# Weight tiles from one explicit list, two ahead, and the down-projection sums in another stage

## The chip, the core and the metric

The kernel runs on one core of a Trainium2 chip. Its time is the device time of one execution in microseconds (us), the median of several runs. The engines are TensorE (PE, matmuls), VectorE (DVE), ScalarE (ACT), GpSimd (POOL) and SyncE (SP). Here SP issues every DMA, in one queue.

## The reference

One decoder layer on x of 2048 tokens by 1024, in float32:

```python
n = rms_norm(h, norm1_w);  z = n @ w_in            # q, k, v, g_lr, g_out, su, sv
o = gla_chunked(q, k, v, log_a(g_lr))              # 4 heads, chunks of 64, state carried on
o_gla = rms_norm(o, gla_norm_w) * silu(g_out)
o_sg  = gelu(su) * (tril(W_s) @ layer_norm(gelu(sv)) + b)   # chunks of 128
h = h + concat(o_gla, o_sg) @ w_out
n2 = rms_norm(h, norm2_w)
h = h + (silu(n2 @ w_ffn_gate) * (n2 @ w_ffn_up)) @ w_ffn_down   # D_FF = 2816
out = rms_norm(h, final_norm_w)
```

## The kernel before

Tokens are worked in four blocks of 512 (`blk` 0 to 3); two blocks make a pass `s`. A pass runs `mix` and `project` for its first block, the same for its second, then `gate_up` and `down` for both blocks together.

A product in float32 is three matmuls (`mm3`, L112) of operands split in a high and a low part: `split` (L92) makes the high part with a cast on ACT and the low part with a subtraction on DVE. `load_w` (L101) loads a weight tile of 128 x 1024 into one of three raw buffers (`rawp`) and splits it into two of eight buffers (`wp`): four tiles may be there at once.

Large products are done by a scheme with seven block products in place of eight, which needs sums and differences of blocks of both operands. For the value and gate products of blocks 1 to 3 (`pair_product`, L200) the sums of weights are in the DRAM tensor `vd`, those of the activations come from `Halves.make` (L159). For the down projection (`down`, L870) the weight sums are in `td`. For gate and up (`gate_up`, L798) they are made as they are needed (`Weights.prep`), up to six products ahead of the one that PE does (`AHEAD`), in 154 products per pass.

`mix` (L414) does in this order: the first columns of sv with the gate's low rank (`tok_group`), k and q (`col_pair` twice), the rest of sv (`second_half`), v and g_out (two `tok_group` in block 0, `pair_product` in blocks 1 to 3), and su in two pairs (`col_pair`). `project` (L703) multiplies by w_out in two halves of columns. Between the products stand the chunk steps of the linear attention (`chunks`, L520; four per block, each with eight state updates and two masked copies on DVE), the layer norm (`sv_norm`), and the attention's output (`attend`).

The program is written as one stream. Side work is held in generators in the list `bg`, and `tick()` (L66) advances each by one step; it is called after each k tile, in `pair_product` after each of the 14 weight tiles. `finish(g)` runs a generator to its end. From that stream each engine gets a fixed list of instructions, made before the run: an instruction written earlier has precedence, but one written later may be put ahead where its inputs and buffers are free sooner. In the run every engine works through its list in order.

The sums of weights in DRAM are made by `weight_sums` (L389): 15 jobs, four for `vd` and eleven for `td`. Each loads four blocks of 128 x 512, does four subtractions on DVE (L403 to L406) and stores the result (L407). It starts after 8 ticks and then does one job every four ticks, so that it runs beside blocks 0 and 1. Its tiles come from the pool `big` (16 buffers). The pool `nwp` has two buffers of 128 x 1024; it holds norm weights and one temporary of `Halves`.

Before, a tile of weights is loaded where it is used: in `tok_group` at the head of each k step, in `pair_product` by `load(m, kk)`, and for `col_pair` both tiles together ahead of the product. The one tile that is loaded earlier by hand is the first of w_out (`pre`, L695).

Of the kernel before, what the change touches and what calls it, by code (L numbers as in the profile page):

```python
# [8 lines left out]
F32 = mybir.dt.float32  # L9
# [4 lines left out]
ALU = mybir.AluOpType  # L14

P = 128
D = 1024
T = 2048
NB = 512
TT = NB // P  # L20
KD = D // P
# [12 lines left out]
def hybrid_block(ctx, tc, x, norm1_w, w_in, w_gate_up, b_gate_up, gla_norm_w, sg_ln_w, sg_ln_b,  # L34
# [41 lines left out]
    def start(g):  # L76
        bg.append(g)
        return g


    half = const.tile([P, 4], F32, name="half")
# [115 lines left out]
            kh, t = {1: (0, 0), 2: (1, 0), 4: (1, 2)}[m]  # L197
            return self.act(4 * kh + k, (t + th) * P, (t + th + 1) * P)

    def pair_product(load, left, order, bank, drain):  # L200

        acc = {}
        for m in order:
            key = bank[m]
            first = key not in acc
            if first:
                acc[key] = [ps(), ps()]
            for kk in range(2):
                hi, lo = load(m, kk)
                for th in range(2):  # L210
                    for j in range(2):
                        mm3(acc[key][th], left(m, 2 * kk + j, th), (hi[:, j, :], lo[:, j, :]),
                            first and kk + j == 0, kk + j == 2, True)
                    if kk:
                        drain(m, th, acc[key][th])
                tick()

    def row_tiles(u):

# [34 lines left out]
        return load_w([w[k0 * P:(k0 + kk) * P, c0:c0 + c].rearrange("(k p) c -> p k c", p=P) for c0, c in col_list], kk,  # L254
                      sum(c for _, c in col_list))

    def tok_group(w, col_list, act, ks=2, order=None, outer=None, done=None, before=None, ws=None, hook=None, pre=None):

        n = sum(c for _, c in col_list)
        order = order or list(range(0, act.nk, ks))  # L260
        acc = [None] * TT

        def load(k0):
            return tok_load(w, col_list, k0, min(ks, act.nk - k0))

        def products(t, k0, hi, lo):
            if acc[t] is None:
                acc[t] = ps()
            for j in range(hi.shape[1]):
                mm3(acc[t][:, :n], act(k0 + j, t * P, (t + 1) * P), (hi[:, j, :], lo[:, j, :]),  # L270
                    k0 == order[0] and j == 0, k0 == order[-1] and j == hi.shape[1] - 1)

        if outer:
            ws = ws or [load(k0) for k0 in order]
            for ts in outer:
                for k0, (hi, lo) in zip(order, ws):
                    if hook:
                        hook(ts[-1], k0)
                    for t in ts:
                        products(t, k0, hi, lo)  # L280
                for t in ts:
                    done(t, acc[t])
                tick()
        else:
            for k0 in order:
                if before and k0 in before:
                    finish(before[k0])
                hi, lo = pre.pop(k0) if pre and k0 in pre else load(k0)
                for t in range(TT):
                    products(t, k0, hi, lo)  # L290
                    if k0 == order[-1]:
                        done(t, acc[t])
                tick()

    def col_load(w, c0):
        return [load_w([w[k0 * P:(k0 + 4) * P, c0:c0 + 2 * P].rearrange("(k p) c -> p k c", p=P)], 4, 2 * P) for k0 in (0, 4)]

    def col_pair(ws, act, a=0, b=NB):

        acc = [ps(), ps()]  # L300
        for i, (hi, lo) in enumerate(ws):
            for k in range(4):
                for c in range(2):
                    cs = slice(c * P, (c + 1) * P)
                    mm3(acc[c][:, :b - a], (hi[:, k, cs], lo[:, k, cs]), act(4 * i + k, a, b), i + k == 0, i == 1 and k == 3)
            tick()
        return acc
# [78 lines left out]
            nc.tensor.matmul(o, lhsT=ones[0:1, :], rhs=bs_bc[:, g, :], start=False, stop=True)  # L386
        nc.vector.tensor_copy(sgb, pb.rearrange("p (a b) -> p a b", b=P))

    def weight_sums():  # L389

        def blocks(w, r, c):
            return [w[r[i] * P:(r[i] + 1) * P, c[j]:c[j] + 512] for i in range(2) for j in range(2)]

        jobs = [(blocks(w_in, (k, 4 + k), (C_V, C_GOUT)), vd[:, k]) for k in range(4)]
        jobs += [(blocks(w_d, (2 * j, 2 * j + 1), (0, 512)), td[:, j]) for j in range(NF // 2)]
        for _ in range(8):
            yield
        for srcs, dst in jobs:
            t = bigt(F32, "wsum")
            for i, src in enumerate(srcs):  # L400
                nc.sync.dma_start(t[:, i], src)
            b11, b12, b21, b22 = (t[:, i] for i in range(4))
            nc.vector.tensor_tensor(b11, b12, b11, ALU.subtract)  # L403
            nc.vector.tensor_tensor(b12, b22, b12, ALU.subtract)
            nc.vector.tensor_tensor(b22, b22, b11, ALU.subtract)
            nc.vector.tensor_tensor(b21, b21, b22, ALU.subtract)  # L406
            nc.sync.dma_start(dst.rearrange("m p d -> p m d"), t)  # L407
            for _ in range(4):
                yield

    start(constants())
    start(weight_sums())

    def mix(blk, nT, first_w):  # L414

# [53 lines left out]
        g_dec = start(decay())  # L469


        ak = col_pair(col_load(w_in, 256), nT)
        finish(g_dec)
        for p in range(2):
            nc.vector.tensor_tensor(ei[:, p, :], ak[p], ei[:, p, :], ALU.mult)
# [15 lines left out]

        for hh in range(2):
            nc.gpsimd.memset(left[other(hh), hh], 0.0)
        aq = col_pair(col_load(w_in, 0), nT)
        for p in range(2):
            for hh in range(2):
                rows = mine(hh)
# [88 lines left out]

        if halves is None:
            tok_group(w_in, [(C_V, 512)], nT, done=lambda t, acc: nc.scalar.copy(v[:, t, :], acc))
            g_chunks = chunks_start()
            second_half()  # L590
            g_svn = start(sv_norm())
            gw = bigt(F32, "gw")
            tok_group(w_in, [(C_GOUT, 512)], nT, done=gate_done)
        else:
            second_half()
            g_svn = start(sv_norm())
            finish(g_half)
            gw = bigt(F32, "gw")
            right_of = {1: (0, C_V), 2: (4, C_V), 3: (4, C_GOUT)}
            started = []  # L600

            def load(m, kk):
                if m in right_of:
                    k0, c0 = right_of[m]
                    return tok_load(w_in, [(c0, 512)], k0 + 2 * kk, 2)
                i = {5: 0, 7: 1, 4: 2, 6: 3}[m]
                return load_w([vd[i, 2 * kk:2 * kk + 2].rearrange("k p c -> p k c")], 2, 512)

            def drain(m, th, acc):
                lo, hi = th, 2 + th  # L610
                if m == 1:
                    nc.scalar.copy(v[:, lo, :], acc)
                elif m == 2:
                    nc.vector.tensor_tensor(v[:, lo, :], acc, v[:, lo, :], ALU.add)
                elif m == 7:
                    nc.scalar.copy(gw[:, hi, :], acc)
                elif m == 6:
                    nc.scalar.copy(v[:, hi, :], acc)
                elif m == 4:
                    nc.vector.tensor_tensor(v[:, hi, :], acc, v[:, hi, :], ALU.add)  # L620
                    if th:
                        started.append(chunks_start())
                elif m == 5:
                    nc.vector.tensor_tensor(gw[:, hi, :], acc, gw[:, hi, :], ALU.add)
                    nc.scalar.activation(gw[:, hi, :], gw[:, hi, :], AF.Silu)
                    gate_scale(hi)
                else:
                    gate_done(lo, acc)

            pair_product(load, halves, (1, 2, 7, 6, 4, 5, 3), {1: 0, 6: 0, 5: 0, 3: 0, 2: 1, 7: 2, 4: 2}, drain)  # L630
            g_chunks = started[0]
        finish(g_chunks)
        finish(g_svn)
# [56 lines left out]
                split(h, l, mx)  # L690

        for i in range(2):
            ws = col_load(w_in, C_SU + i * 2 * P)
            if i == 1:
                pre = {4: tok_load(w_out, [(0, 512)], 4, 2)}  # L695
            gate_pair(i, col_pair(ws, nT))
        return mixT, g_att, pre, hx

    def residual(hx, dh, acc, t):
        sl = hx[t][:, dh * 512:(dh + 1) * 512]  # L700
        nc.vector.tensor_tensor(sl, acc, sl, ALU.add)

    def project(blk, hx, mixT, g_att, pre, put, outer, ahead=None):  # L703

        def norm2_put(t, xs):
            yield
# [16 lines left out]

        gens = []
        n2w = norm_w(norm2_w[0])
        tok_group(w_out, [(0, 512)], mixT, order=[4, 0, 6, 2], before={0: g_att}, pre=pre, done=lambda t, acc: residual(hx, 0, acc, t))
        tok_group(w_out, [(512, 512)], mixT, outer=outer, done=out_done, hook=hook)
        if not outer:
            start(norm_rows(hx, put, n2w))
# [269 lines left out]
    for s in range(2):  # L999

        blk = 2 * s
        mixT, g_att, pre, hx = mix(blk, nT, first_w)
        first_w = None
        hx1 = dma_x(x2, blk + 1)
        nT = Act(KD, "nT")
# [7 lines left out]
            if t == TT - 1:  # L1013
                nc.sync.dma_start(bd[i], b1[i])

        project(blk, hx, mixT, g_att, pre, put_first, None)
        finish(g_n1)


        blk += 1  # L1020
        mixT, g_att, pre, hx = mix(blk, nT, None)
        b1 = [bigt(F32, f"b1{i}") for i in range(2)]
        b2 = [None, None]
        tm = {}
# [30 lines left out]

        start(first_operands())
        ahead, run = gate_up(s, tm)
        gens = project(blk, hx, mixT, g_att, pre, put_second, ((0, 1), (2,), (3,)), ahead)

        def last_operands():  # L1060
            for g in gens:
# [9 lines left out]

        start(last_operands())
        d_start, d_run = down(s)
        run(d_start())
        tm.clear()

        nxt = {}
# [39 lines left out]
```

## Time and profile before

| | us |
|---|---|
| median of 3 runs | 2050.57 |
| range of the runs | 2049.33 to 2052.22 |
| profiled execution, device time | 2049.34 |
| its span, first to last instruction | 2047.6 |
| PE busy | 1987.0 |
| DVE busy | 1503.1 |
| ACT busy | 892.6 |

A row of the profile names the line, the engine and the operation, what it writes and from what (`wlo<-raw,whi` is the low part of a weight tile). PEclk is the granted clock of TensorE as a share of full speed (2.4 GHz; the other level is 1.2 GHz, shown as 0.5 where it lasts). A matmul's own time is longer than its distance to the next, since matmuls overlap. Because L94, L95 and L115 to L117 are in helpers, rows are told apart by their tiles. In the run, pass 0 has block 0 up to about 200 us, block 1 to 395, gate and up to 815, and down to 1045; the second pass follows in the same order.

### The profile page before, as it was taken

How to read it: one execution, taken by the hardware profiler on the slowest of the kernel's cores; microseconds unless marked ns; L12 is line 12 of the kernel's file. 1: busy time of each engine (PE TensorE's matmuls, PEld its weight loads, DVE VectorE, ACT ScalarE, POOL GpSimd, SP SyncE). 2: the span in 40 equal slices, each digit the busy share in tenths (PEclk: the TensorE clock that was granted, in tenths of full speed). 3: DMA queues.
4: the chain of work that ended last, by engine and by line, in shares of the span. 5: the costliest groups of instructions: out<-in, count | busy, mean ns of one | idle time of the engine just before them, and what ended most of it. 6: DMA issues, size and time to landing. Idle time of an engine off the chain costs nothing. (4 is left out here: it accounts for less than half of the span.)

```text
span 2047.6 us, 26475 instructions
## 1 busy us (share of the span) xinstructions
PE 1987.0 (97%) x9837; PEld 1652.4 (81%) x9837; DVE 1503.1 (73%) x2485; ACT 892.6 (44%) x1454; POOL 88.5 (4%) x102
## 2 busy tenths in 40 slices
PE   7999979999999999999999999999999999999997
PEld 6888967878888888888878788788888888888886
DVE  5677886698877877655797668767987787775466
ACT  4444625354333333443565447345433333334334
POOL 1011100000000000000110001000000000000000
PEclk9999998999999999999999999999999999999999
DMA  6666687423332333865655534723332232367545
GB/s 191 198 215 213 227 266 257 166 98 104 116 104 90 125 101 124 294 199 185 241 172 156 174 105 156 209 99 108 103 124 92 96 122 93 103 213 258 196 160 180
DMA packets 204575, 329.27 MB, mean 161 GB/s; under 512 B 15719, under 2 KB 94237, under 8 KB 203422
## 3 DMA queue, kind: packets, MB, share of 16 engines
q1 hardware_dynamic: 204446, 327.58, 48.8%
q8 instruction: 77, 1.26, 0.3%
q14 instruction: 52, 0.43, 0.1%
HBM read 246.27 MB, written 77.07 MB: 158 GB/s over the span
## 5 line engine op out<-in xcount | busy, mean ns | idle before, releaser
L94 ACT CAST whi<-raw 128x1024 fp32r<-128x1024 f32 (+2 forms) x209 | 210.6, 1010 | 350.0 <-PE ps L116 131.8
L95 DVE TENSOR_TENSOR wlo<-raw,whi 128x1024 fp32r<-128x1024 f32 (+2 forms) x209 | 243.2, 1171 | 141.0 <-ACT whi L94 130.0
L115 PE MATMUL ps<-whi,aop 128*128 128x512 f32 x552 | 215.1, 390 | 0.0
L117 PE MATMUL ps<-whi,aop 128*128 128x512 f32 x552 | 214.9, 389 | 0.0
L116 PE MATMUL ps<-wlo,aop 128*128 128x512 f32 x552 | 214.8, 389 | 0.0
L94 ACT CAST op<-sw 128x512 fp32r<-128x512 f32 x176 | 107.5, 621 | 182.1 <-DVE sw L757 155.3
L95 DVE TENSOR_TENSOR aop<-raw,aop 128x1024 fp32r<-128x1024 f32 x84 | 95.2, 1134 | 96.4 <-ACT aop L94 96.0
L95 DVE TENSOR_TENSOR op<-sw,op 128x512 fp32r<-128x512 f32 x176 | 120.6, 687 | 42.8 <-ACT op L94 42.3
L94 ACT CAST aop<-raw 128x1024 fp32r<-128x1024 f32 x84 | 82.1, 979 | 136.4 <-DMA raw<-ad 135.2
L115 PE MATMUL ps<-whi,nTl 128*128 128x512 f32 (+2 forms) x392 | 128.4, 328 | 3.4 <-DVE nTl L95 3.4
L116 PE MATMUL ps<-wlo,nTh 128*128 128x512 f32 (+2 forms) x392 | 126.6, 323 | 0.2 <-DVE wlo L95 0.2
L117 PE MATMUL ps<-whi,nTh 128*128 128x512 f32 (+2 forms) x392 | 126.6, 323 | 0.0
L116 PEld LDWEIGHTS ps<-wlo,aop 128*128 128x128 f32 x552 | 103.6, 188 | 21.6
L115 PEld LDWEIGHTS ps<-whi,aop 128*128 128x128 f32 x552 | 103.6, 188 | 21.4
L117 PEld LDWEIGHTS ps<-whi,aop 128*128 128x128 f32 x552 | 103.6, 188 | 21.3
L115 PE MATMUL ps<-nTh,wlo 128*128 128x512 f32 x256 | 106.1, 415 | 15.0 <-DVE wlo L95 15.0
L782 ACT COPY p<-ps 128x512 f32<-128x512 f32 x88 | 51.6, 588 | 148.9 <-PE ps L117 143.3
L95 DVE TENSOR_TENSOR op<-raw,op 128x512 fp32r<-128x512 f32 x132 | 88.8, 687 | 31.5 <-ACT op L94 31.0
L122 POOL TENSOR_TENSOR st<-st,half 128x1 f32<-128x1 f32 x48 | 41.6, 875 | 1471.4 <-DVE st L121 1444.8
L115 PE MATMUL ps<-whi,mixTl 128*128 128x512 f32 x256 | 101.9, 398 | 1.8 <-DVE mixTl L95 1.7
L116 PE MATMUL ps<-nTl,whi 128*128 128x512 f32 x256 | 103.4, 404 | 0.0
L117 PE MATMUL ps<-nTh,whi 128*128 128x512 f32 x256 | 103.2, 403 | 0.0
(253 smaller groups left out, 4966.2 us busy)
## 6 DMA issues: line engine op xcount, KB each, us to landing
raw<-ad SPq DMA_DIRECT2D x70, 512.0 KB, 3.8
raw<-in_w_in_dram SPq DMA_DIRECT2D x66, 512.0 KB, 4.6
raw<-in_w_ffn_gate_dram SPq DMA_DIRECT2D x44, 512.0 KB, 3.7
raw<-in_w_ffn_up_dram SPq DMA_DIRECT2D x44, 512.0 KB, 3.8
raw<-td SPq DMA_DIRECT2D x40, 512.0 KB, 4.2
ad<-cg SPq DMA_DIRECT2D x66, 256.0 KB, 2.0
ad<-cs SPq DMA_DIRECT2D x22, 768.0 KB, 3.5
hx<-in_x_dram SPq DMA_DIRECT2D x32, 512.0 KB, 7.1
```

What stands on the lines that cost most here:

```text
L94: nc.scalar.copy(hi, src)
L95: nc.vector.tensor_tensor(lo, src, f32(hi), ALU.subtract)
L115: nc.tensor.matmul(o, lhsT=ll, rhs=rh, start=first, stop=False, skip_group_check=shared)
L116: nc.tensor.matmul(o, lhsT=lh, rhs=rl, start=False, stop=False, skip_group_check=shared)
L117: nc.tensor.matmul(o, lhsT=lh, rhs=rh, start=False, stop=last, skip_group_check=shared)
L122: nc.gpsimd.tensor_tensor(dst, dst, half[:, :k], ALU.pow)
L782: nc.scalar.copy(t[m], o)
```

## The change

Four things are done.

- The weight tiles of a block's `mix` and `project` stand in one list (`block_tiles`), in the order of use, put into `queue` for both blocks of a pass at the pass's start. `next_w()` loads until three tiles are ready and gives out the first, so a tile's load and split are written two tiles ahead of its matmuls, across the borders of products and of the two blocks. `pre` is gone.
- `pair_product` calls `tick()` once for each of its seven block products, not after each of the 14 tiles.
- The value sums (`value_sums`) start after two ticks and take seven ticks a job: one after each load, one after each two subtractions, one after the store.
- The down sums (`down_sums`) are started with the first pass's `gate_up`. There are 22 jobs of half the columns (256), seven ticks each, 154 in all; their tiles come from `nwp`.

```diff
+    AHEAD_W = 2
+    queue, ready = [], []
+    def next_w():
+        while queue and len(ready) <= AHEAD_W:
+            ready.append(queue.pop(0)())
+        return ready.pop(0)
...
 pair_product:
             for kk in range(2):
-                hi, lo = load(m, kk)
+                hi, lo = next_w()
...
-                tick()
+            tick()
...
 tok_group:
-                hi, lo = pre.pop(k0) if pre and k0 in pre else load(k0)
+                hi, lo = ws.pop(0) if ws else next_w()
...
 col_pair:
-        for i, (hi, lo) in enumerate(ws):
+        for i in range(2):
+            hi, lo = next_w()
...
-    def weight_sums():
...
+    def sums_of(t, srcs, dst):
+        for i, src in enumerate(srcs):
+            nc.sync.dma_start(t[:, i], src)
+            yield
+        b11, b12, b21, b22 = (t[:, i] for i in range(4))
+        nc.vector.tensor_tensor(b11, b12, b11, ALU.subtract)
+        nc.vector.tensor_tensor(b12, b22, b12, ALU.subtract)
+        yield
+        nc.vector.tensor_tensor(b22, b22, b11, ALU.subtract)
+        nc.vector.tensor_tensor(b21, b21, b22, ALU.subtract)
+        yield
+        nc.sync.dma_start(dst, t)
+        yield
+    def value_sums():
+        for _ in range(2):
+            yield
+        for k in range(4):
+            srcs = [w_in[r * P:(r + 1) * P, c:c + 512] for r in (k, 4 + k) for c in (C_V, C_GOUT)]
+            yield from sums_of(bigt(F32, "wsum"), srcs, vd[:, k].rearrange("m p d -> p m d"))
+    def down_sums():
+        for j in range(NF // 2):
+            for i in range(2):
+                srcs = [w_d[(2 * j + c) * P:(2 * j + c + 1) * P, l * 512 + i * 256:l * 512 + (i + 1) * 256]
+                        for c in range(2) for l in range(2)]
+                t = nwp.tile([P, D], F32, name="nw", tag="nw").rearrange("p (a b) -> p a b", a=4)
+                yield from sums_of(t, srcs, td[:, j, :, i * 256:(i + 1) * 256].rearrange("m p d -> p m d"))
...
+    OUT_ORDER = [4, 0, 6, 2]
+    VG_ORDER = (1, 2, 7, 6, 4, 5, 3)
+    def block_tiles(blk, first):
...
+        tiles = [] if first else tok_tiles(w_in, first_cols, 3)
+        tiles += col_tiles(w_in, 256) + col_tiles(w_in, 0)
+        second = tok_tiles(w_in, [(C_SV + 256, 256)], 4)
+        if blk == 0:
+            tiles += tok_tiles(w_in, [(C_V, 512)]) + second + tok_tiles(w_in, [(C_GOUT, 512)])
+        else:
+            tiles += second + [lambda m=m, kk=kk: vg(m, kk) for m in VG_ORDER for kk in range(2)]
+        for i in range(2):
+            tiles += col_tiles(w_in, C_SU + i * 2 * P)
+        return tiles + tok_tiles(w_out, [(0, 512)], order=OUT_ORDER) + tok_tiles(w_out, [(512, 512)])
...
     for s in range(2):
         blk = 2 * s
-        mixT, g_att, pre, hx = mix(blk, nT, first_w)
+        queue.extend(block_tiles(blk, first_w) + block_tiles(blk + 1, None))
+        mixT, g_att, hx = mix(blk, nT, first_w)
...
         d_start, d_run = down(s)
+        if s == 0:
+            g_sums = start(down_sums())
         run(d_start())
+        if s == 0:
+            finish(g_sums)
```

## Rows read from the trace of the kernel before

**Rows 1.** The page: busy time, share of the span and instructions of each engine.

```profile
PE 1987.0 (97%) x9837; PEld 1652.4 (81%) x9837; DVE 1503.1 (73%) x2485; ACT 892.6 (44%) x1454; POOL 88.5 (4%) x102
```

**Rows 2.** Table by stage: length, busy time (count) by engine, granted clock, DMA share, GB/s.

```profile
260.00:320.00 60.00, 43.85 (x267) 33.65 (x268) 47.26 (x94) 16.89 (x22) 1.96 (x2) 0.84 0.90 294
...
392.00:440.00 48.00, 45.88 (x197) 36.16 (x197) 45.17 (x74) 29.08 (x53) 1.40 (x2) 0.96 0.47 152
440.00:500.00 60.00, 60.00 (x266) 49.69 (x265) 56.06 (x92) 26.73 (x46) 0.00 (x0) 1.00 0.38 122
500.00:800.00 300.00, 300.00 (x1326) 248.49 (x1325) 230.68 (x365) 109.06 (x189) 0.00 (x0) 1.00 0.33 107
...
1000.00:1056.00 56.00, 51.18 (x279) 44.50 (x278) 50.98 (x91) 35.32 (x71) 11.93 (x14) 0.97 0.69 233
...
1118.00:1146.00 28.00, 23.06 (x163) 17.80 (x164) 23.32 (x51) 7.76 (x10) 0.00 (x0) 0.88 0.78 207
...
1277.00:1330.00 53.00, 48.23 (x302) 38.41 (x302) 41.23 (x82) 20.74 (x26) 2.01 (x2) 0.94 0.68 199
```

**Rows 3.** The same table for two shorter stretches of block 1.

```profile
268.00:278.00 10.00, 6.81 (x23) 5.12 (x22) 6.87 (x10) 4.25 (x7) 0.00 (x0) 0.83 0.70 237
303.00:322.00 19.00, 10.63 (x31) 7.92 (x32) 13.25 (x24) 4.22 (x5) 0.00 (x0) 0.55 0.91 305
```

**Rows 4.** Rows in order of time, PE: start, us, what; in brackets the wait before.

```profile
411.77 0.73 PE L115 MATMUL ps<-t5h,op 128*128 128x512 f32 x2 [1.24 <-ACT t5h L94]
...
1052.70 0.79 PE L115 MATMUL ps<-nTh,wlo 128*128 128x512 f32 x1 [4.82 <-DVE wlo L95]
...
1322.58 0.77 PE L115 MATMUL ps<-nTh,wlo 128*128 128x512 f32 x1 [3.60 <-DVE wlo L95]
```

**Rows 5.** Rows in order of time, DVE, starts of block 2 and end of block 3's product.

```profile
1051.44 1.21 DVE L95 TENSOR_TENSOR wlo<-raw,whi 128x1024 fp32r<-128x1024 f32 x1
...
1302.73 2.99 DVE L536 SCALAR_TENSOR_TENSOR right<-right,dec,ps 64x128 f32<-64x128 f32 x8
1305.64 0.92 DVE L547 COPY_PREDICATED left<-keep,ps 64x256 f32<-64x256 int32 x2
...
1320.02 1.28 DVE L581 TENSOR_TENSOR gw<-gw,gnw 128x512 f32<-128x512 f32 x2
1321.22 3.48 DVE L95 TENSOR_TENSOR wlo<-raw,whi 128x1024 fp32r<-128x1024 f32 x3
```

**Rows 6.** Rows in order of time, ACT, of the same two places.

```profile
1039.69 1.04 ACT L94 CAST whi<-raw 128x1024 fp32r<-128x1024 f32 x1
...
1304.42 1.04 ACT L94 CAST whi<-raw 128x1024 fp32r<-128x1024 f32 x1 [2.97 <-PE ps L116]
```

**Rows 7.** Rows in order of time, SP's queue (DMA issues), block 1.

```profile
223.65 0.34 SPq L88 DMA_DIRECT2D nw<-in_final_norm_w_dram  x1
...
249.51 2.07 SPq L106 DMA_DIRECT2D raw<-vd  x2
...
263.71 1.91 SPq L106 DMA_DIRECT2D raw<-vd  x2
270.90 0.36 SPq L407 DMA_DIRECT2D td<-wsum  x1
```

**Rows 8.** Waits of SP's queue from 200 to 420: us in total, times, longest.

```profile
SPq L407 <- DVE wsum L406: 36.5, 6, 9.1
```

**Rows 9.** One tile, wsum: ns min/median/max, first and last start; the last line is its DMAs'.

```profile
L401 SPq DMA_DIRECT2D wsum<-in_w_ffn_down_dram x44: 418/460/1471, 149.3 to 400.8; - x44
...
L406 DVE TENSOR_TENSOR wsum<-wsum x15: 672/685/693, 70.4 to 411.0; 128x512 f32<-128x512 f32 x15
...
DMA to landing us min/median/max: 3.0/5.3/8.1
```

**Rows 10.** The page's groups: busy us, mean ns of one, idle before.

```profile
L95 DVE TENSOR_TENSOR wlo<-raw,whi 128x1024 fp32r<-128x1024 f32 (+2 forms) x209 | 243.2, 1171 | 141.0 <-ACT whi L94 130.0
...
L95 DVE TENSOR_TENSOR op<-sw,op 128x512 fp32r<-128x512 f32 x176 | 120.6, 687 | 42.8 <-ACT op L94 42.3
```

More of the change, by code (lines that the diff above doesn't have):

```diff
@@ L198, in __call__, with pair_product @@
             return self.act(4 * kh + k, (t + th) * P, (t + th + 1) * P)
-    def pair_product(load, left, order, bank, drain):
+    def pair_product(left, order, bank, drain):
         acc = {}
@@ L255, in tok_load, with tok_tiles, tok_group @@
                       sum(c for _, c in col_list))
-    def tok_group(w, col_list, act, ks=2, order=None, outer=None, done=None, before=None, ws=None, hook=None, pre=None):
+    def tok_tiles(w, col_list, ks=2, order=None):
+        return [lambda k0=k0: tok_load(w, col_list, k0, min(ks, KD - k0)) for k0 in order or range(0, KD, ks)]
+    def tok_group(w, col_list, act, ks=2, order=None, outer=None, done=None, before=None, ws=None, hook=None):
         n = sum(c for _, c in col_list)
@@ L261, in tok_group @@
         acc = [None] * TT
-        def load(k0):
-            return tok_load(w, col_list, k0, min(ks, act.nk - k0))
         def products(t, k0, hi, lo):
@@ L273, in tok_group @@
         if outer:
-            ws = ws or [load(k0) for k0 in order]
+            ws = ws or [next_w() for k0 in order]
             for ts in outer:
@@ L293, in tok_group, with col_tiles, col_pair @@
                 tick()
-    def col_load(w, c0):
-        return [load_w([w[k0 * P:(k0 + 4) * P, c0:c0 + 2 * P].rearrange("(k p) c -> p k c", p=P)], 4, 2 * P) for k0 in (0, 4)]
-    def col_pair(ws, act, a=0, b=NB):
+    def col_tiles(w, c0):
+        return [lambda k0=k0: load_w([w[k0 * P:(k0 + 4) * P, c0:c0 + 2 * P].rearrange("(k p) c -> p k c", p=P)], 4, 2 * P)
+                for k0 in (0, 4)]
+    def col_pair(act, a=0, b=NB):
         acc = [ps(), ps()]
-        for i, (hi, lo) in enumerate(ws):
+        for i in range(2):
+            hi, lo = next_w()
             for k in range(4):
@@ L387, in constants @@
         nc.vector.tensor_copy(sgb, pb.rearrange("p (a b) -> p a b", b=P))
-    def weight_sums():
[L391 to L396, printed above, removed]
-            yield
[L398 to L409, printed above, removed]
@@ L411, in hybrid_block @@
-    start(constants())
-    start(weight_sums())
+    def sums_of(t, srcs, dst):
+        for i, src in enumerate(srcs):
+            nc.sync.dma_start(t[:, i], src)
+            yield
+        b11, b12, b21, b22 = (t[:, i] for i in range(4))
[7 more added lines that the diff above has]
+        yield
@@ new lines, in hybrid_block, with vg @@
+    start(constants())
+    start(value_sums())
+    OUT_ORDER = [4, 0, 6, 2]
+    VG_ORDER = (1, 2, 7, 6, 4, 5, 3)
+    def block_tiles(blk, first):
+        def vg(m, kk):
+            at = {1: (0, C_V), 2: (4, C_V), 3: (4, C_GOUT)}.get(m)
+            if at:
+                return tok_load(w_in, [(at[1], 512)], at[0] + 2 * kk, 2)
+            return load_w([vd[{5: 0, 7: 1, 4: 2, 6: 3}[m], 2 * kk:2 * kk + 2].rearrange("k p c -> p k c")], 2, 512)
+        tiles = [] if first else tok_tiles(w_in, first_cols, 3)
[8 more added lines that the diff above has]
+        return tiles + tok_tiles(w_out, [(0, 512)], order=OUT_ORDER) + tok_tiles(w_out, [(512, 512)])
@@ L469, in mix @@
         g_dec = start(decay())
-        ak = col_pair(col_load(w_in, 256), nT)
+        ak = col_pair(nT)
         finish(g_dec)
@@ L493, in mix @@
             nc.gpsimd.memset(left[other(hh), hh], 0.0)
-        aq = col_pair(col_load(w_in, 0), nT)
+        aq = col_pair(nT)
         for p in range(2):
@@ L598, in mix @@
             gw = bigt(F32, "gw")
-            right_of = {1: (0, C_V), 2: (4, C_V), 3: (4, C_GOUT)}
             started = []
[L602 to L607, printed above, removed]
             def drain(m, th, acc):
@@ L628, in drain @@
                     gate_done(lo, acc)
-            pair_product(load, halves, (1, 2, 7, 6, 4, 5, 3), {1: 0, 6: 0, 5: 0, 3: 0, 2: 1, 7: 2, 4: 2}, drain)
+            pair_product(halves, VG_ORDER, {1: 0, 6: 0, 5: 0, 3: 0, 2: 1, 7: 2, 4: 2}, drain)
             g_chunks = started[0]
@@ L692, in mix @@
         for i in range(2):
[L693 to L697, printed above, removed]
+            gate_pair(i, col_pair(nT))
+        return mixT, g_att, hx
     def residual(hx, dh, acc, t):
@@ L701, in residual, with project @@
         nc.vector.tensor_tensor(sl, acc, sl, ALU.add)
-    def project(blk, hx, mixT, g_att, pre, put, outer, ahead=None):
+    def project(blk, hx, mixT, g_att, put, outer, ahead=None):
         def norm2_put(t, xs):
@@ L725, in project @@
         n2w = norm_w(norm2_w[0])
-        tok_group(w_out, [(0, 512)], mixT, order=[4, 0, 6, 2], before={0: g_att}, pre=pre, done=lambda t, acc: residual(hx, 0, acc, t))
+        tok_group(w_out, [(0, 512)], mixT, order=OUT_ORDER, before={0: g_att}, done=lambda t, acc: residual(hx, 0, acc, t))
         tok_group(w_out, [(512, 512)], mixT, outer=outer, done=out_done, hook=hook)
@@ L1014, in put_first @@
                 nc.sync.dma_start(bd[i], b1[i])
-        project(blk, hx, mixT, g_att, pre, put_first, None)
+        project(blk, hx, mixT, g_att, put_first, None)
         finish(g_n1)
         blk += 1
-        mixT, g_att, pre, hx = mix(blk, nT, None)
+        mixT, g_att, hx = mix(blk, nT, None)
         b1 = [bigt(F32, f"b1{i}") for i in range(2)]
@@ L1057, in hybrid_block @@
         ahead, run = gate_up(s, tm)
-        gens = project(blk, hx, mixT, g_att, pre, put_second, ((0, 1), (2,), (3,)), ahead)
+        gens = project(blk, hx, mixT, g_att, put_second, ((0, 1), (2,), (3,)), ahead)
         def last_operands():
```

## The prediction

> **What bounds the kernel now.** I read the page first, then a table by stage, then single rows. TensorE is busy for 1987.0 of 2047.6 us [rows 1], so only the other 60.6 us and the matmuls that ran at the lower clock can be won. In the table [rows 2] the reader is to look for length minus PE busy, and for a granted clock under 1.00. From 500 to 800 us (first gate-and-up stage) PE is busy throughout; there 1326 matmuls took 300 us, 0.226 us each, so one block product of 12 takes 2.71 us, and DVE has 23% to spare. The losses stand in five stretches:
>
> - 260:320, the value-and-gate product of block 1: 60 - 43.85 = 16.15 us without a matmul, at a mean clock of 0.84. Of the slowed time [rows 3] the second row has 10.63 us of matmuls, of which 90% at 1.2 GHz instead of 2.4 (the mean is 0.55): half of that, 4.8 us, is lost. The first row has 34% of 10 us: 1.7 us (all of it busy, after the wait). Together 22.6 us.
> - 1118:1146 and 1277:1330, the same product in blocks 2 and 3: 4.94 and 4.77 us without a matmul. The clocks 0.88 and 0.94 mean 6.7 and 6.4 us at the lower level, which cost at most half, 3.3 us each, and less by the part in which PE waited anyway; I take 2.8. Together 15.3 us.
> - 1000:1056, the start of block 2: 4.82 us, in one wait [rows 4], and 3.4 us at the lower clock (0.97), taken as 1.5: 6.3 us.
> - 392:440, the start of the first gate-and-up stage: 2.12 us, most of it one wait for t5 [rows 4], and 3.8 us at the lower clock (0.96), so 1.9: 4.0 us.
>
> What PE waits for at nearly all of these places is a `wlo`, the low part of a weight tile, which DVE makes [rows 4]. The DVE rows [rows 5] show why it is late. DVE was not short of data: ScalarE made the high part of the first su tile of block 3 at 1304.42 [rows 6], and DVE made the low part only at 1321.22, after four chunk steps (each 2.99 + 0.92 us) and the gate scalings that stand ahead of it in its order. At the start of block 2 it is the same: high part at 1039.69 [rows 6], low part at 1051.44 [rows 5], with sums of the normed halves in between. So the order on DVE makes the wait there, not the transfer.
>
> Block 1 loses 7 to 8 us more than its sisters because the weight sums run beside it. SP's rows [rows 7] show its queue standing from 265.6 to 270.90 until DVE had done the four subtractions of a sum; behind that store stood the next raw tile. In 200:420 SP waited 36.5 us so, in six waits [rows 8].
>
> **The change, part by part.**
>
> *Tiles two ahead.* Each `next_w` writes the load and split of the tile two places further on. That alters no count of instructions, only where the splits stand in the orders of SP, ACT and DVE. At the start of block 2 the first k tile is now written with the second tile of the first group, before the halves sums of the following ticks: the 4.82 us wait and its slow clock should go but for some 0.5 us: -5.8 us. At the ends of the products the first su tile comes before m = 3's drains and two of the chunk steps: the 3.60 us wait for `wlo` [rows 4] goes. Next late is PSUM: chunk steps 2 and 3 take four buffers each, all eight, so the su accumulators wait for step 2's eight state updates (2.99 us) on DVE. I leave 3 to 4 us of the 7.6 in each of blocks 2 and 3: -8.2 us in all. Bounds: 0, if that DVE work merely stalls PE one instruction later, and -15.3, if nothing is left.
>
> The trace has ACT and DVE work in a fixed order: the split of 1321.22 was possible from 1305.5 and still came last [rows 5, 6]. The Trainium skill (TensorE: Matmul & The Clock Gate, Architectural detail) calls these two engines strict first-in, first-out queues, and by that a split moved ahead of a drain holds the drain when its transfer is late, which speaks against this edit. The trace agrees on the order; were one 5.3 us hold, as of SP in rows 7, put on a drain in each of blocks 1 to 3, the sum below would be 16 us smaller. I don't follow it, since the tiles wanted earlier come from inputs that need nothing but a raw buffer.
>
> *One tick per m in place of two in the product.* The chunk steps, `sv_norm` and `kend` spread over more matmuls; the last chunk step falls behind the product. No instruction is added. It costs the PSUM wait above and is counted there.
>
> *The sums leave blocks 0 and 1.* Eleven jobs of four 0.685 us subtractions [rows 9], 30 us of DVE, 44 loads and 11 stores go. PE had next to no loss in block 0, so nothing is won there; but the last job, whose fourth subtraction starts at 411.0 [rows 9], stands ahead of the t5 sum for which PE waited: 2.7 us. The four value jobs stay, with a tick after each load: the last store comes with the 30th tick, the last of block 0, before the reads at 249.51 [rows 7].
>
> But they may not leave wholly. SP issued the final norm weights, written at the start of `down` for use at its end, at 223.65 [rows 7], as soon as one of the two `nw` buffers was free: orders here follow free buffers, not the place in the source. The new sums take their tiles from these two buffers, ahead of that load. So I expect half-size jobs from 223 us on, in one buffer, until the other, with the norm2 weights, comes free at the end of block 1. One job needs four loads of 0.46 us issue each [rows 9], a landing, 1.8 us of DVE and a store: some 13 to 15 us each by the 5.3 us median landing [rows 9], so up to 12 of the 22 before the gate-and-up stage. Their DVE work stands behind everything else that is ready, each instruction is shorter, and tiles two ahead give SP's queue 5.4 us (two tiles of 12 matmuls) of cover against holds of about that length. I take 8 us as what block 1 loses (4 like its sisters, 4 from these jobs): 22.6 - 8 = -14.6 us. Bounds: -19 (as its sisters after the change) and 0.
>
> *The sums in the gate-and-up stage.* 88 subtractions of 128 x 256. No such row exists; with 0.687 us for 512 columns and 1.171 for 1024 [rows 10] a line gives 0.44 us; half of the 512 row, 0.34, and all of it, 0.685, are the ends. So 30 to 60, I take 39 us of DVE, of which the part not done in block 1 falls here. The stage has 154 products, 417 us; DVE idles 23% of it outside its first 60 us [rows 2], some 80 us. Products are prepared six ahead, 16 us of cover. SP gets 88 loads and 22 stores, about 0.4 us each, 45 us over these 420 and the time before. I put the cost at 3 us here and for small new waits elsewhere. Bounds: 0, and 39 if all of it stalled PE. At the very start DVE is full (45.17 of 48 us in 392:440), and there the old job (2.7 us) goes and at most two new ones (3.5 us) come: of the 4.0 us lost I let 1.4 go.
>
> Sum: -14.6 - 8.2 - 5.8 - 1.4 + 3 = -27.0 us. The profiled execution took 2049.34 us (span 2047.6 and 1.7 around it): 2022.3. The median of the runs shown is 1.2 us above it, so I forecast **2024 us**.
>
> **Rivals.**
>
> *The sums stay in block 1.* If the early `nw` jobs hold SP's queue as the old ones did, block 1 keeps its 22.6 us. For it speaks the row at 223.65; against it the halved bytes and DVE work and the cover of two tiles. 2024 + 14.6 = 2038 us.
>
> *The ends of the products don't move.* DVE works from 1302.73 to the wait at 1322.58 [rows 4, 5] while PE has some 15 us of matmuls there; a new order leaves its sum as it is. Then blocks 2 and 3 give nothing: 2024 + 8.2 = 2032 us. Against it: what DVE does last now, step 3 and two scalings, isn't wanted by the next matmuls.
>
> *All goes.* If stalls shrink enough that the clock holds, only the unavoidable stays: 22.6 + 15.3 + 6.3 + 4.0 = 48 us could go, less some 6 us of PSUM waits: 2050.6 - 42 = 2008 us. Against it: it needs all five places at once.
>
> *Slower.* In the first gate-and-up stage the sums' work on DVE lands on PE's path: a subtraction waits on DVE for loads that stand in SP's queue behind a raw tile without a buffer, and every preparation behind it is late. That stage's DVE is full for its first 60 us (56.06 of 60 in 440:500), which speaks for it; 300 us without one PE wait [rows 2] speak against. It decides from 27 us on, 1.2 us for each of the 22 jobs, and at its full 39 us gives 2024 + 39 = 2063 us.
>
> **How the numbers follow.** Forecast 0.44 (its own range 2016 to 2031), sums stay 0.17, ends don't move 0.17, all goes 0.10, no net change 0.04, slower 0.08. The first four are faster by more than 0.2% (4 us, about what a measurement of this kernel can tell from no change): 0.88; within it 0.04; slower 0.08. The range runs from 2010, near the end at which all goes, to 2041, above the end at which the sums stay; outside it I leave the rest of these and the slower case.
>
> **What would show it.** Right: no wait for `wlo` near 1050 and at the ends of the three products, a PE busy time some 10 us lower (less slowed time), four to five us lost at each end, in rows that name PSUM or DVE's state updates; `nw` loads of the down weights from about 223 us on. The sums' own step is wrong if no such load stands before 390. The gate-and-up step is wrong if PE has a wait between 440 and 800. The forecast as a whole is wrong if block 1's product still loses over 15 us, or if ACT's splits wait for their raw tiles with drains behind them.

## The result, and the profile after

The changed kernel took 2025.15 us where the kernel before took 2050.12 in the same runs: the ratio is 0.9871 (95% interval 0.9852 to 0.9890), 25 us less. One of the four executions of the changed kernel took 4715.83 us, for a reason that is not known, and the ratio is without it. The forecast was 2024 us. Its profiled execution took 2024.96 us, with a span of 2023.0.

The page's first part after: PE is busy 9.9 us less than in [rows 1] with the same 9837 matmuls. Most of that is slowed time that is gone: 31.0 us of matmuls ran at 1.2 GHz before and 14.8 us after, at twice their time. The rest of the gain is shorter waits.

```profile
PE 1977.1 (98%) x9837; PEld 1646.7 (81%) x9837; DVE 1503.8 (74%) x2529; ACT 890.4 (44%) x1454; POOL 92.2 (5%) x102
```

The table by stage, to be read beside [rows 2] (length, busy time by engine, granted clock, DMA share, GB/s; everything from 260 us on lies 0 to 25 us earlier):

```profile
260.00:320.00 60.00, 54.35 (x356) 43.49 (x356) 48.81 (x105) 23.64 (x35) 3.34 (x3) 0.94 0.77 230
...
500.00:800.00 300.00, 300.00 (x1326) 248.39 (x1325) 241.15 (x394) 110.73 (x192) 0.00 (x0) 1.00 0.43 139
...
1100.00:1130.00 30.00, 27.41 (x231) 21.61 (x230) 27.52 (x56) 11.84 (x18) 0.00 (x0) 0.94 0.79 222
...
1255.00:1310.00 55.00, 53.03 (x354) 42.86 (x353) 45.35 (x98) 24.57 (x36) 4.04 (x4) 1.00 0.65 200
```

Block 1's product has 54.35 us of matmuls in 260:320 where it had 43.85. The ends of the products in blocks 2 and 3 (1100:1130 and 1255:1310) lack 2.6 and 2.0 us where they lacked 4.9 and 4.8. In gate-and-up DVE has 241 us of work in 300 where it had 231, and PE still does not wait.

PE's rows at three of the five places, to be read beside [rows 4]; in brackets the wait:

```profile
292.06 0.33 PE L584 MATMUL ps<-left,eu 64*64 64x64 f32 x2 [1.87 <-DVE right L577]
293.57 1.12 PE L584 MATMUL ps<-left,eu 64*64 64x64 f32 x14 [1.19 <-DVE right L577]
296.20 0.77 PE L124 MATMUL ps<-whi,hop 128*128 128x512 f32 x1 [1.52 <-DVE gw L657]
...
306.33 0.50 PE L124 MATMUL ps<-nTh,wlo 128*128 128x512 f32 x1 [0.76 <-DVE right L577]
...
1037.71 0.50 PE L124 MATMUL ps<-nTh,wlo 128*128 128x512 f32 x1 [1.65 <-DVE wlo L104]
...
1050.88 0.70 PE L492 MATMUL ps<-glrT,wup 96*128 96x512 f32 x2 [1.50 <-DVE glrT L477]
...
1298.77 0.50 PE L124 MATMUL ps<-nTh,wlo 128*128 128x512 f32 x1 [1.44 <-DVE right L577]
```

The waits for a `wlo` at the ends of the products are gone. What is late there now is `right`, the state update of a chunk step. It reads one of the eight PSUM buffers that the chunk steps and su's accumulators share, so the wait (1.44 us at 1298.77) is read as one for that buffer. At the start of block 2 the 4.82 us wait became 1.65 us, and a second of 1.50 us came in behind it, for `glrT`.

DVE's rows at the end of block 3's product, beside [rows 5]:

```profile
1287.65 1.21 DVE L104 TENSOR_TENSOR wlo<-raw,whi 128x1024 fp32r<-128x1024 f32 x1
...
1294.91 1.21 DVE L104 TENSOR_TENSOR wlo<-raw,whi 128x1024 fp32r<-128x1024 f32 x1
...
1297.61 2.63 DVE L577 SCALAR_TENSOR_TENSOR right<-right,dec,ps 64x128 f32<-64x128 f32 x7
```

ACT's for the same place, beside [rows 6]:

```profile
1285.43 1.05 ACT L103 CAST whi<-raw 128x1024 fp32r<-128x1024 f32 x1 [2.79 <-DVE right L577]
1288.15 1.04 ACT L103 CAST whi<-raw 128x1024 fp32r<-128x1024 f32 x1 [1.67 <-PE ps L125]
```

The low part of the first su tile now comes at 1287.65, 1.2 us after its high part (1285.43 + 1.05), with the updates of three chunk steps still to come; that of the second comes at 1294.91, ahead of the last two of them (from 1296.64 on). Before, 16 us lay between the two parts.

SP's queue in block 1, beside [rows 7], its waits from 200 to 420 (us in total, times, longest), beside [rows 8], and the down sums' tile (ns min/median/max, first and last start), beside [rows 9]:

```profile
225.93 1.77 SPq L403 DMA_DIRECT2D nw<-in_w_ffn_down_dram  x4
...
390.20 2.33 SPq L403 DMA_DIRECT2D nw<-in_w_ffn_down_dram  x5
```

```profile
SPq L403 <- DMA td<-nw: 22.4, 9, 4.7
SPq L412 <- DVE nw L410: 20.3, 8, 4.9
```

```profile
L403 SPq DMA_DIRECT2D nw<-in_w_ffn_down_dram x88: 328/430/1017, 225.9 to 563.7; - x88
...
L406 DVE TENSOR_TENSOR nw<-nw x22: 391/419/426, 232.1 to 563.9; 128x256 f32<-128x256 f32 x22
```

The down sums begin at 225.93, 2 us after the place at which the final norm weights were loaded before, and not with the gate-and-up stage, whose first product starts at 386.65. Ten of the 22 jobs had their loads issued by 390, and SP still stood for 20 us on their stores and for another 22 us on a buffer whose store had not landed.

### The profile page after: what moved, and what is told of

Read it like the earlier page. It is cut to its first block, busy times and chain, and to the rows that moved or that the text cites. A ratio compares the mean times of both kernels' runs of the same rounds, so it can differ in the third digit from the quotient of the medians.

```text
span 2023.0 us, 26612 instructions
## 1 busy us (share of the span) xinstructions
PE 1977.1 (98%) x9837; PEld 1646.7 (81%) x9837; DVE 1503.8 (74%) x2529; ACT 890.4 (44%) x1454; POOL 92.2 (5%) x102
```

## The experiments

My theory: the list takes away waits that the order on DVE makes (start of block 2, ends of the products), and the sums' leaving takes away most of block 1's loss, which SP's holds make. The rivals: one of the two parts alone makes all of the gain. Each experiment was timed beside runs of the kernel before on the same chip; ratios are to those.

**Each part alone.** First the list, with the weight sums and the ticks of before:

```diff
-    start(value_sums())
+    start(weight_sums())        # 15 whole jobs, as before
...
-            tick()
+                tick()          # after each tile, as before
...
-            g_sums = start(down_sums())
```

> The weight list two ahead alone: weight sums as before (15 whole jobs beside blocks 0 and 1), a tick after each tile as before. If the order of splits on DVE made the waits at the start of block 2 and at the ends of the products in blocks 2 and 3, these go as in the changed kernel (about 3 and 9 us), and block 1 keeps most of its 22.6 us, for the sums' stores still hold SP's queue: 2050 - 12 to - 18 = 2032 to 2038 us, with SP waits on wsum near 30 us from 200 to 420. If the tiles ahead cover SP's holds as well, all of the gain comes with them: about 2026 us. If the gain came from the sums alone: 2048 to 2052.

2021.62 us, ratio 0.9846 (0.9825 to 0.9868): the list alone makes all of the gain of the whole change, and the expectation that block 1 keeps most of its loss failed. PE's rows show what is left, and SP's row its wait on the sums in 200:420:

```profile
269.84 0.50 PE L125 MATMUL ps<-wlo,hop 128*128 128x512 f32 x1 [2.45 <-DVE wlo L104]
...
303.61 0.50 PE L124 MATMUL ps<-nTh,wlo 128*128 128x512 f32 x1 [1.07 <-DVE wlo L104]
...
1037.05 0.79 PE L124 MATMUL ps<-nTh,wlo 128*128 128x512 f32 x1 [3.57 <-DVE wlo L104]
```

```profile
SPq L418 <- DVE wsum L417: 27.4, 6, 8.2
```

So 27.4 us of SP's holds (36.5 before) are still there. But the two large waits of before are gone, 4.92 and 2.97 us:

```profile
309.07 0.80 PE L116 MATMUL ps<-wlo,hop 128*128 128x512 f32 x1 [4.92 <-DVE wlo L95]
...
316.68 0.76 PE L115 MATMUL ps<-nTh,wlo 128*128 128x512 f32 x1 [2.97 <-DVE wlo L95]
```

The first was for the last tile of the value-and-gate product, the second for su's first; the slowed clock of 303:322 [rows 3] lies around them. Now the rows of ACT, DVE and PE, before, for that last tile and for the earlier wait of 3.19 us, at which the prediction saw SP's hold:

```profile
264.50 1.05 ACT L94 CAST whi<-raw 128x1024 fp32r<-128x1024 f32 x1 [6.30 <-DMA raw<-vd]
...
290.05 1.04 ACT L94 CAST whi<-raw 128x1024 fp32r<-128x1024 f32 x1 [4.18 <-DMA raw<-in_w_in_dram]
```

```profile
270.18 0.69 DVE L406 TENSOR_TENSOR wsum<-wsum 128x512 f32<-128x512 f32 x1
...
271.38 3.49 DVE L95 TENSOR_TENSOR wlo<-raw,whi 128x1024 fp32r<-128x1024 f32 x3
...
307.81 1.21 DVE L95 TENSOR_TENSOR wlo<-raw,whi 128x1024 fp32r<-128x1024 f32 x1
```

```profile
272.66 0.50 PE L116 MATMUL ps<-wlo,hop 128*128 128x512 f32 x1 [3.19 <-DVE wlo L95]
```

The tile that PE got at 272.66 had its high part at 265.55, before SP stood still; its low part, the first of the three at 271.38, came 5.8 us later, behind four subtractions of a sum (2.7 us) and other work of DVE. The raw tile behind the store of 270.90 [rows 7] is a later one, and PE did not wait for it: its next wait is at 291. The last tile had its high part at 291.09 and its low part at 307.81, behind the last three chunk steps and four more subtractions (2.7 us between 299.08 and 303.05). So in both places the sums stood in PE's way on DVE. With the list, ACT's and DVE's rows are these (and SP's for su's first two tiles):

```profile
259.76 1.05 ACT L103 CAST whi<-raw 128x1024 fp32r<-128x1024 f32 x1 [2.62 <-DMA raw<-vd]
```

```profile
268.57 3.49 DVE L104 TENSOR_TENSOR wlo<-raw,whi 128x1024 fp32r<-128x1024 f32 x3
...
292.44 1.21 DVE L104 TENSOR_TENSOR wlo<-raw,whi 128x1024 fp32r<-128x1024 f32 x1
```

```profile
267.82 0.36 SPq L418 DMA_DIRECT2D td<-wsum  x1
...
291.38 0.93 SPq L115 DMA_DIRECT2D raw<-in_w_in_dram  x2
```

The wait of 2.45 us at 269.84 is of the same kind: high part at 260.81, low part at 268.57 behind four subtractions, and SP's hold until 267.82 isn't in it. But the last tile's low part now comes at 292.44 in place of 307.81, ahead of the last two chunk steps, and su's first two raw tiles are issued at 291.38, ahead of the loads of x; before, the first was issued at 306.29, behind a sum's store at 303.07 and these loads. How much of the 2.97 us SP's hold at that store made, and how much of the last tile's lateness an earlier one, is not shown.

Then the sums alone, weights loaded as before:

```diff
-    start(weight_sums())
+    start(value_sums())
...
+        if s == 0:
+            g_sums = start(down_sums())
```

> The new sums alone (value sums from the third tick, down sums in half-size jobs in the norm weights' two buffers): weights loaded where they are used, a tick after each tile. If the sums' leaving makes block 1's gain, block 1 loses 10 to 14 us in place of 22.6 and the start of gate-and-up 2 in place of 4, while the wait of 4.8 us at the start of block 2 and the ends of the products in blocks 2 and 3 stay: 2036 to 2041 us. If the list is what saves block 1: 2046 to 2052. If the sums are all of it: 2026.

2040.02 us, ratio 0.9941 (0.9920 to 0.9963), 11 us less than before, as expected if the sums' leaving makes block 1's gain. PE's rows show the waits for low parts of the first tiles where they were:

```profile
307.31 0.47 PE L115 MATMUL ps<-nTh,wlo 128*128 128x512 f32 x1 [3.04 <-DVE wlo L95]
...
1128.48 0.76 PE L115 MATMUL ps<-nTh,wlo 128*128 128x512 f32 x1 [3.59 <-DVE wlo L95]
```

The table for block 1's product, the list alone and then the sums alone (before, PE was busy for 58.66 of the 75 us):

```profile
255.00:330.00 75.00, 69.15 (x438) 54.68 (x437) 62.07 (x124) 31.48 (x59) 5.81 (x6) 0.98 0.84 276
```

```profile
255.00:330.00 75.00, 67.86 (x410) 53.78 (x409) 57.19 (x124) 29.59 (x51) 5.30 (x5) 0.93 0.72 222
```

With slowed time at half its length, block 1 lost about 23 us before, loses 7.6 with the list alone (5.85 and 1.7) and 11.5 with the sums alone (7.1 and 4.4). The list takes away 15 us, the sums' move 11, and they do not add up: most of the loss needed both, sums beside block 1 and splits written late. So 29 and 11 us by themselves are 25 together. On top of the list the sums' move, as it is in this change, is worth nothing that shows, as the next run says.

**The tick.** The changed kernel with a tick after each of the 14 tiles:

```diff
-            tick()
+                tick()
```

> The changed kernel with a tick after each of the 14 tiles of the product again. If PSUM is what is late at its end because two chunk steps come together behind m = 3, the waits of su's accumulators on the state updates (0.8 to 1.5 us, three times) go and waits inside the product (matmuls of chunk steps on state updates, 0.5 to 2.5 us) come back: 2022 to 2028 us, no difference that stands clear. If the spreading of the chunk steps is what freed DVE at the ends, the 3.6 us waits come back in blocks 1 to 3: 2033 to 2040.

> The changed kernel once more, beside the variants. If the tick per block product costs what the PE waits on state updates at the ends of the three products show (some 5 us with the slowed clock), it is 2024 to 2026 us, 3 to 5 above the same kernel with a tick per tile (2021.6). If those two were the same and the difference lay in the runs, it is 2020 to 2023.

2021.57 us, ratio 0.9842 (0.9819 to 0.9866), and the changed kernel again, on another chip, 2024.19 us, ratio 0.9865 (0.9848 to 0.9882). The intervals overlap: a difference of 3 us is not shown, though the profile with 14 ticks has none of the su waits on `right`. With 14 ticks on both sides, list and new sums (2021.57) equal list and old sums (2021.62).

**The amount ahead.** The list with the old sums and 14 ticks, with 0, 1 and 3 tiles ahead:

```diff
-    AHEAD_W = 2
+    AHEAD_W = 0                 # in the others 1 and 3
```

> As e1_list_only, with no tile ahead: each tile is loaded where it is used (now also the second of a col_pair, and the first of w_out). If the two tiles ahead make the gain of the list, all of it goes, and a little more since two places had their tiles ahead before: 2048 to 2060 us. If the gain came from the list in itself, from leaving out `pre` and loading col_pair's tiles one by one: about 2022.

> As e1_list_only with one tile ahead. If what counts is only that the first tile of a product comes before the DVE work that stands at the border, one tile is enough for the ends of the products in blocks 2 and 3, while SP's holds in block 1 (5 us) are longer than one tile's 2.7 us of matmuls: 2024 to 2034 us. If two are needed everywhere: 2035 to 2045. If one does all: 2020 to 2023.

> As e1_list_only with three tiles ahead, which takes all eight split buffers. If more cover helps, the 2.45 us wait for a low part in block 1 and the 3.57 us at the start of block 2 go: 2015 to 2019 us. If the buffers bind, since the split of the third tile waits for the matmuls before, there is no difference: 2020 to 2024. If splits held up on ACT by their transfers hold drains: 2026 or more.

| tiles ahead | us | ratio (95%) |
|---|---|---|
| 0 | 2052.60 | 1.0000 (0.9986 to 1.0014) |
| 1 | 2039.54 | 0.9939 (0.9925 to 0.9954) |
| 2 | 2021.62 | 0.9846 (0.9825 to 0.9868) |
| 3 | 2028.83 | 0.9892 (0.9879 to 0.9905) |

With none ahead, all waits are back, as PE's rows say, and the list by itself is worth nothing:

```profile
320.00 0.47 PE L124 MATMUL ps<-nTh,wlo 128*128 128x512 f32 x1 [3.77 <-DVE wlo L104]
...
1058.64 0.79 PE L124 MATMUL ps<-nTh,wlo 128*128 128x512 f32 x1 [6.71 <-DVE wlo L104]
```

With one, the time is that of the expectation that two are needed everywhere. With three, it is that of the third expectation, but not by drains on ACT. At the start of block 2 PE waits for small copies that stand behind sums, and splits, on DVE; PE's rows, then DVE's:

```profile
1048.42 0.68 PE L468 MATMUL ps<-ident,glr 128*96 128x128 f32 x2 [2.17 <-DVE glr L461]
...
1057.94 0.70 PE L484 MATMUL ps<-glrT,wup 96*128 96x512 f32 x2 [1.73 <-DVE glrT L469]
```

```profile
1046.91 1.21 DVE L192 TENSOR_TENSOR nw<-nw,hs 128x1024 f32<-128x1024 f32 x1
1048.04 0.17 DVE L459 COPY glr<-glrhi 128x16 f32<-128x16 f32 x1
```

These two waits, 3.90 us, stand where two tiles ahead had the one of 3.57 us, so with the slowed clock they explain about 1 us of the 7 by which three are slower than two (2028.83 less 2021.62). The rest is spread over several places, and its cause is not shown.

**The early sums.** The changed kernel (one tick per block product) with the final norm weights taken first, so that they hold one of the two buffers from 226 us on:

```diff
+        fw = norm_w(final_norm_w)
         if s == 0:
             g_sums = start(down_sums())
...
         def run(nxt):
-            fw = norm_w(final_norm_w)
```

> The changed kernel with the final norm weights taken ahead of the down sums, so that they hold one of the two buffers from about 225 us on, and no down sum can begin before the other is free at the end of block 1. If the ten or so early jobs cost block 1 some 4 of the 8.4 us that it still loses, and gate-and-up takes 22 jobs in one buffer without a PE wait: 2019 to 2022 us. If the early jobs are free where they are: 2024 to 2027, and the first 60 us of gate-and-up, where DVE is full, may lose 1 to 3 us: up to 2029.

2018.37 us, ratio 0.9832 (0.9809 to 0.9855); its interval just touches those of the changed kernel (from 0.9848 and 0.9852 on). PE's rows, and DVE's at the start of gate-and-up:

```profile
299.52 0.50 PE L124 MATMUL ps<-nTh,wlo 128*128 128x512 f32 x1 [1.44 <-DVE right L577]
...
414.71 0.50 PE L124 MATMUL ps<-t3h,op 128*128 128x512 f32 x1 [2.95 <-DVE op L104]
```

```profile
407.82 0.41 DVE L406 TENSOR_TENSOR nw<-nw 128x256 f32<-128x256 f32 x1
408.16 2.48 DVE L104 TENSOR_TENSOR t3l<-b,t3h 128x512 fp32r<-128x512 f32 x4
```

Block 1 now has su's wait on a state update and nothing else: 1.8 us (1.44 and a further 0.32) where the changed kernel lost 8. In exchange the first sum's subtraction stands ahead of `t3l` at 407.82, and 2.95 us are lost with 3.4 us of slowed clock behind it; that the sums make this wait, the run after the next shows. With a tick after each tile besides:

> The changed kernel with the final norm weights taken first and a tick after each tile. If the two costs are separate: the waits of su on state updates (1.4 and 0.3 us, three times) go, waits of chunk steps of 0.5 to 1.2 us come: 2015 to 2018 us. If the early sums were what made room for either, it stays at 2018 to 2021. The wait of 2.95 us at the start of gate-and-up stays in both.

2018.55 us, ratio 0.9836 (0.9818 to 0.9854): the tick adds nothing that shows here. Then the down sums 24 ticks later as well:

```diff
     def down_sums():
+        for _ in range(24):
+            yield
```

> As e5_both_edits, with the down sums written 24 ticks later, so that in the first 60 us of gate-and-up, where DVE is full, they stand behind its other work. If the first sum's subtractions make the waits there (1.17 and 2.95 us and 3.4 us of slow clock), these shrink to the 1.6 us that the second pass has without sums: 3 to 4 us less than e5_both_edits, 2011 to 2015 us. If DVE is simply full there: no difference.

2012.83 us, ratio 0.9813 (0.9794 to 0.9832): the lowest median of the complete kernels, 39 us less than before and 11 less than the changed kernel on the same chip (2024.19), clear of its interval. Against the run just before, the intervals overlap; but in PE's rows its 2.95 us wait is gone, and the start of gate-and-up has one wait, of 1.57 us. Its four executions lie between 2009.24 and 2016.77, and the profiled one, 2010.32, is among the quicker. The sums' tile, and the table for block 1's product and gate-and-up:

```profile
L403 SPq DMA_DIRECT2D nw<-in_w_ffn_down_dram x88: 333/423/504, 382.9 to 730.4; - x88
...
L406 DVE TENSOR_TENSOR nw<-nw x22: 418/425/432, 447.4 to 737.9; 128x256 f32<-128x256 f32 x22
```

```profile
255.00:315.00 60.00, 58.99 (x393) 47.61 (x392) 47.40 (x99) 28.38 (x47) 4.03 (x4) 1.00 0.65 196
...
500.00:800.00 300.00, 300.00 (x1326) 248.39 (x1325) 253.44 (x436) 106.86 (x188) 0.00 (x0) 1.00 0.56 178
```

No sum is loaded before 382.9 or subtracted before 447.4; block 1's product has 1.0 us without a matmul, at full clock, and in gate-and-up DVE does 253 us of work in 300 with no wait of PE. With three tiles ahead:

> As e6_sums_later with three tiles ahead. If the waits at the start of block 2 (1.6 and 1.5 us) are a matter of cover, 2009 to 2012 us; if the eight split buffers bind, as e6_sums_later, 2011 to 2015; if ACT and DVE spend themselves on tiles that aren't due, above 2016.

2015.21 us, ratio 0.9826 (0.9813 to 0.9838): no gain, and not clearly a loss.

**No down sums at all**, on the changed kernel with 14 ticks; four of the seven down products multiply plain blocks of the weights, so that part is left out:

```diff
-        right.update({m: td[i].rearrange("j p d -> p j d") for i, m in enumerate((5, 7, 4, 6))})
+        right.update({5: wd[1, 1], 7: wd[0, 1], 4: wd[0, 0], 6: wd[1, 0]})
```

> The changed kernel with a tick after each tile, and without the down sums: the four products that need them multiply plain blocks of the down weights, so this part of the output is left out. What all 22 jobs cost on top of the list, in block 1 and in gate-and-up. If the list hides them but for block 1's early jobs: 2010 to 2015 us (block 1 loses some 2 us, gate-and-up 1.6). If they cost nothing beyond what e3 shows: 2019 to 2022. If the sums cost more than their order can save (DVE or DMA work in itself): under 2008.

2012.90 us, ratio 0.9820 (0.9804 to 0.9835). By the medians the 22 jobs as changed cost some 9 us (2021.57 less 2012.90) by where they stand, but the intervals of the two ratios overlap, so the size is uncertain. Where e6_sums_later puts them they cost nothing that can be seen: 2012.83.

## Why the prediction was right, and where it was not

*Time:* right, by a sum in which one term's cause was only half seen and errors in others partly cancel.

*Block 1 (-14.6, 8 left):* the size is right. After, it loses 5.65 us in waits and some 2.4 us of slowed matmuls (6.8 us at the lower clock). Of the reasoning, part held.

- "Block 1 loses 7 to 8 us more than its sisters" compares 22.6 us with the 15.3 that both sisters lose together. Against either one it is 15 us more.
- That the weight sums beside it make this extra loss is borne out: with the sums moved and nothing else, 11 us of it go. But the list alone takes away 15 with the sums still there, and the expectation that block 1 would then keep most of its loss failed.
- The way was wrong. SP's hold of rows 7 was offered as the proof, but the tile behind that store made no wait of PE; the 3.19 us wait was for a tile whose high part was ready at 265.55 and whose low part stood behind the subtractions on DVE. It was the order on DVE here too.

The early jobs that I put at 4 us cost about 6 (8 less the 1.8 of the run with the final norm weights first). That they would run in block 1 from 223 us on, from the load of the final norm weights, was right to 2 us.

*Ends of the products (-8.2, 7.1 left):* right in cause, and near in size: 6.3 left. 2.6 us and 1.7 of slowed time are left in block 2, 2.0 in block 3, and most of it (1.8 us in each) is the wait for the chunk steps' state updates.

*Start of block 2 (-5.8, 0.5 left):* the cause is right (none ahead: 6.71 us of wait there), the size is not: 3.15 us are left, and the sign "no wait for `wlo` near 1050" did not come, since 1.65 us of it is one. In the repeat of the changed kernel the wait for `wlo` is 3.01 us, with slowed clock around it. I didn't look at what is late next: `glrT` on DVE, behind the same sums of halves.

*Start of gate-and-up (2.6 left):* 1.8 left, in three waits.

*Sums in gate-and-up (+3 with small waits elsewhere):* gate-and-up itself costs nothing after 440, and a subtraction took 0.42 us where I took 0.44. The small new waits are more than 3: PE's other new or longer waits add up to 4.4 us (0.56 at 111, 0.68 more at 165, 0.40 each at 348 and 1341, 1.74 near 1000, 0.6 more near 1990), and 6.8 us at the lower clock at 34 and 1996 cost 3.4 more. That these come from the sums is not shown.

*The sum:* forecast -27.0, measured 24.4 less (2049.34 less 2024.96). Read place by place from the rows, with slowed time at half its length, the gains are 14.8, 8.9, 3.2 and 1.8 us and the new losses 7.8: 21 us. Some 3 us of the gain stand in none of these readings.

*The rivals.* "The sums stay in block 1" was true of ten of the 22 jobs, but not at its price. "Slower" needed a wait of PE between 440 and 800, and there is none. The Trainium skill (TensorE: Matmul & The Clock Gate, Architectural detail) calls ACT and DVE strict first-in, first-out; by that a split that waits for its transfer holds the drains behind it. The trace agrees as far as that ACT stood on a raw tile in block 1, with drains later in its order:

```profile
266.11 1.05 ACT L103 CAST whi<-raw 128x1024 fp32r<-128x1024 f32 x1 [4.80 <-DMA raw<-vd]
```

The prediction had named this as a sign against the whole forecast. But no wait of PE follows from it, and the 16 us of that rival did not come.

Open: whether the tick per block product costs anything, and why one tile ahead covers so little of the ends of the products (1.80 and 2.36 us remain there).

## What to carry to other kernels

Where an instruction stands in an engine's order can cost as much as its data being late (16 us between two parts of one tile, here): look for the time between a tile's first part and its second, and write the load of the next product's first tile in front of the work that drains this one. Two parts of a change that meet in one stretch must each be run alone before either is credited. Work written later is not done later when its buffers are free: to hold it back, hold its buffer.

## What the runs showed that I had not expected

More lookahead is not always better: with the old sums, 0, 1, 2 and 3 tiles gave 2052.6, 2039.5, 2021.6 and 2028.8 us. And 22 jobs with 37 us of DVE work (88 x 0.42) can be free beside a stage whose DVE was already busy for 77%, as far as 2012.83 with them against 2012.90 without can tell (each good to some 4 us), if they stand behind its first 60 us.
